# First FFN over all tile pairs, then mixer and second FFN per tile, with the instruction order fixed by a list scheduler

## The chip, the cores and the metric

The kernel runs on all eight cores of one Trainium2 chip. Each core works on one sequence of the batch, and all run the same program; they share no data. The time of a run is the device time of the slowest core, in microseconds. A profile shows the slowest core of one execution.

The program has two states. In the slow one, the cores of a die, sometimes of both, show a lower granted TensorE clock and the time is some per cent longer. A run counts as slow when one die is over 1% longer than the other at a lower clock, or when it is over 1.5% above the fastest of its kernel. The medians given are of all runs of a kernel, and where slow ones are among them, the median of the fast ones alone lies at most 1.3 us lower (for the kernel before, 15 us: 3,231.0).

## The reference

One sequence is 4,096 tokens of width 1,024. Cut to what matters:

```python
mod = silu(c) @ w_mod + b_mod               # c: one vector per sequence; 9 parts of 1,024
h = rmsnorm(x, g1) * (1 + sc1) + sh1
x = x + 0.5 * gt1 * swiglu(h, w_ffn1_in, w_ffn1_out)        # hidden width 2816
h = rmsnorm(x, g_mix) * (1 + sc2) + sh2
u_val, u_gate, u_x, u_y = split(h @ w_in)                    # 4 x 512
y_conv = silu(layernorm(causal_conv31(u_val * sigmoid(u_gate))))   # depthwise
xr = causal_conv4(u_x); r = sigmoid(xr @ w_a + b_a); i = sigmoid(xr @ w_i + b_i)
a = exp(8 * r * logsigmoid(lam)); h_t = a_t * h_{t-1} + sqrt(1 - a_t^2) * i_t * xr_t
x = x + gt2 * (concat(y_conv, gelu(u_y) * h_t) @ w_out)
x = x + 0.5 * gt3 * swiglu(rmsnorm(x, g2) * (1 + sc3) + sh3, w_ffn2_in, w_ffn2_out)
return rmsnorm(x, g_final) * (1 + f_sc) + f_sh               # silu(c) @ w_fmod
```

The convolution and the recurrence carry state along the sequence, so the mixer must go tile by tile. The first FFN depends on no other tile.

## The kernel before

A tile is 512 tokens; there are eight. Activations lie with features on the 128 partitions, so a product is a chain of 128x512 matmuls that accumulate in a PSUM bank. Weights come through four slots of 128 x 8 x 512 bf16 (1 MB). The whole layer is run tile by tile; a second tile is begun early and fills in. Tile 0 loads the fp32 weights with a cast on the POOL queue and writes the bf16 copies back to DRAM for the later tiles.

```python
def issue_slab():                       # cut
    elif tile == 0:                     # fp32 -> bf16 in flight, then written back
        emit(PL, mk(pieces), writes=[r_slot[si]], dma=sem_slot_pl[si], ...)
        emit(SP, mk(back), reads=[r_slot[si]], writes=[r_scr[pos]], dma=sem_wb[si], ...)
    else:
        emit(SP, mk(pieces), reads=[r_scr[pos]], writes=[r_slot[si]], dma=sem_slot[si], ...)

def mod_part(g0, g1):                   # modulation: one-column fp32 matmuls
    ...
    for sub in range(2):
        for kc in range(8):
            h.matmul(ps[:, bank, j:j + 1], lhsT=sf[:, kc, sub * 128:(sub + 1) * 128],
                     rhs=cact[:, kc:kc + 1], start=(kc == 0), stop=(kc == 7))

def rsqrt_chain(buf, res, bank, scale): # rstd of every norm
    E(ACT, ... func=AF.Sqrt, bias=EPS, scale=scale)
    E(DVE, ... h.reciprocal(out=buf[:], in_=buf[:]))

def conv_chunk(c):                      # conv31: 31 diagonal matmuls of 512 columns
    mm_group(b, [(dflat[:, k * 128:(k + 1) * 128], ub[:, c, k:k + T]) for k in range(NCONV)], ...)

def tile_gen(i):                        # cut: one tile, start to end
    norm(s, gs1, sh1); ffn(s, "w1i", "w1o", gth1)
    norm(s, gs2, sh2); mixer(s)
    norm(s, gs3, sh3); ffn(s, "w2i", "w2o", gth3); final norm
```

## Time and profile before

| | before |
|---|---|
| median of the three runs shown with it, two of them slow | 3,331.65 us (3,228 to 3,597) |
| median of all five | 3,246.2 us |
| span of the profiled (fast) execution | 3,239.8 us |
| PE busy | 2,835 us, 88% |

The first view is the table of windows of core 1, for four stretches. Its columns are the stretch, its length, PE's busy time with the number of matmuls in it, the granted TensorE clock, the DMA engines' mean share of busy time, and GB/s.

```profile
core 1: us, PE busy (x), PEclk, DMA share, GB/s
240.00:320.00 80.00, 75.44 (x339) 0.73 1.01 211
880.00:960.00 80.00, 72.16 (x337) 0.65 0.74 195
1040.00:1120.00 80.00, 80.00 (x372) 1.00 0.50 152
1280.00:1360.00 80.00, 80.00 (x372) 1.00 0.48 149
```

An undisturbed stretch holds 372 matmuls in 80 us, or 215.2 ns each, at clock 1.00. That is the rate that everything is measured against. Note that 240 to 320 is "94% busy" and still completes only 339, at clock 0.73: a busy share hides a clock that has dropped, so count matmuls. There the DMA share is at its limit (1.01).

The next lines are groups of instructions: line, engine and operation, output from inputs, shapes, count, then busy us and mean ns, then idle time of the engine before them and what ended most of it.

```profile
L353 PE MATMUL ps<-sb_hb,sb_slab 128*128 128x512 bf16 x7168 | 1603.8, 386 | 185.3 <-ACT sb_hb L428 77.8
...
L371 PE MATMUL ps<-sb_cact,sb_slab 128*128 128x1 f32 x1408 | 293.8, 347 | 41.4 <-DMA sb_slab<-w_mod 33.9
...
L353 PE MATMUL ps<-sb_ub,sb_slab 128*128 128x512 bf16 x992 | 217.3, 379 | 3.3 <-DMA sb_slab<-dcw 3.3
...
L394 DVE RECIPROCAL sb_rstd<-sb_rstd 128x512 f32<-128x512 f32 x32 | 107.3, 3353 | 102.5 <-ACT sb_rstd L392 102.5
```

The second line is the modulation: 1,408 matmuls that make one column each. The fourth is the reciprocal of a 128x512 tile, 3.35 us, in the chain from one norm to the next matmul. The busy time of matmuls in this view is not a cost by itself, because the mean of 386 ns overlaps with neighbours; the rate of 215.2 ns is.

The last is the chain that ended last, as shares of the span by engine.

```profile
PE 71%; DMA 12%; ACT 7%; DVE 6%; issue 3%; SPq 0%; POOL 0%; ACTq 0%; DVEq 0%; POOLq 0%
```

TensorE leads, with 12% of DMA. In the windows, the stretch from 132 to 1,008 us (tile 0 with its casts) has clock 0.81 and DMA share 0.81; the later tiles lose about 45 us each in gaps at norms.

### The profile page before, as it was taken

What the parts mean: (1) busy time and instruction counts of PE and PEld (TensorE: products, weight loads), DVE (VectorE), ACT (ScalarE), POOL (GpSimd) and SP (SyncE); (2) the same over time, 40 slices, a digit from 0 to 9 for tenths busy, and PEclk for the clock granted to TensorE, in tenths of its full rate; (3) what the DMA queues carried; (4) which work ended last, traced back from release to release, by engine and by line L of the source; (5) the groups of instructions that cost most, each with busy time, mean ns of one, the idle gap of its engine ahead of it and who ended that gap; (6) DMA issues with size and microseconds to landing.
All of it is one profiled execution on the core that took longest, in us unless ns stands there. A gap on an engine that the chain in (4) does not pass through costs nothing.

```text
span 3239.8 us, 35643 instructions; the slowest of 8 cores (3213.5 to 3239.8 us)
## 1 busy us (share of the span) xinstructions
PE 2835.0 (88%) x12768; PEld 1413.3 (44%) x12768; DVE 1005.6 (31%) x1411; ACT 937.8 (29%) x1406; POOL 101.4 (3%) x146
## 2 busy tenths in 40 slices
PE   6479998797997999969979999969979999879976
PEld 6136644653572434434434444424424444334433
DVE  0210124243004123254433223355232222554232
ACT  0310215143005132164323223246132321535121
POOL 1000000001000000000000000000000000000000
PEclk9887798689768999989989999989989999989988
DMA  7699469569964465433445555433444644424442
GB/s 179 119 201 220 144 144 227 152 135 193 213 186 143 150 179 149 153 103 116 131 139 156 156 172 149 144 94 117 150 143 150 208 137 147 132 90 136 144 130 85
DMA packets 650859, 487.04 MB, mean 150 GB/s; under 512 B 11712, under 2 KB 637888, under 8 KB 650688
## 3 DMA queue, kind: packets, MB, share of 16 engines
q1 hardware_dynamic: 574944, 405.99, 42.4%
q0 software_dynamic: 75744, 78.78, 13.7%
q8 instruction: 106, 1.74, 0.2%
q14 instruction: 65, 0.53, 0.1%
HBM read 468.21 MB, written 61.73 MB: 164 GB/s over the span
## 4 chain that ended last, share of the span: by engine, by line
PE 71%; DMA 12%; ACT 7%; DVE 6%; issue 3%; SPq 0%; POOL 0%; ACTq 0%; DVEq 0%; POOLq 0%
PE ps L353 62%; PE ps L371 9%; DMA sb_xT<-x 2%; DMA sb_slab<-w_mod 2%; DVE sb_xr L489 1%; DMA sb_slab<-win 1%; DMA sb_slab<-w1i 1%; DMA sb_slab<-w2i 1%; DMA sb_slab<-w1o 1%; ACT sb_hb L428 1%; ACT sb_xsq L410 1%; DVE sb_ntmp L425 1%; DVE sb_rstd L394 1%; DMA b2i<-sb_slab 1%; DMA b1i<-sb_slab 1%
## 5 line engine op out<-in xcount | busy, mean ns | idle before, releaser
L353 PE MATMUL ps<-sb_hb,sb_slab 128*128 128x512 bf16 x7168 | 1603.8, 386 | 185.3 <-ACT sb_hb L428 77.8
L353 PEld LDWEIGHTS ps<-sb_hb,sb_slab 128*128 128x128 bf16 x7168 | 708.8, 99 | 1064.7 <-issue 252.3
L353 PE MATMUL ps<-sb_hid,sb_slab 128*128 128x512 bf16 x2816 | 614.9, 381 | 0.4 <-DMA sb_slab<-w2o 0.4
L448 DVE TENSOR_TENSOR sb_hid<-ps,sb_sgb 128x512 bf16<-128x512 f32 x352 | 240.5, 689 | 890.2 <-PE ps L353 724.8
L446 ACT ACTIVATE sb_sgb<-ps 128x512 f32<-128x512 f32 x352 | 206.0, 595 | 979.0 <-PE ps L353 976.9
L353 PEld LDWEIGHTS ps<-sb_hid,sb_slab 128*128 128x128 bf16 x2816 | 276.5, 98 | 335.9 <-issue 7.1
L371 PE MATMUL ps<-sb_cact,sb_slab 128*128 128x1 f32 x1408 | 293.8, 347 | 41.4 <-DMA sb_slab<-w_mod 33.9
L371 PEld LDWEIGHTS ps<-sb_cact,sb_slab 128*128 128x128 f32 x1408 | 293.8, 326 | 43.5 <-issue 43.2
L410 ACT ACTIVATE sb_xsq<-sb_xT 128x512 bf16<-128x512 f32 x256 | 144.1, 621 | 472.5 <-PE ps L353 207.3
L465 DVE SCALAR_TENSOR_TENSOR sb_xT<-ps,sb_gth,sb_xT 128x512 f32<-128x512 f32 x128 | 96.1, 751 | 498.6 <-PE ps L353 498.6
L353 PE MATMUL ps<-sb_ub,sb_slab 128*128 128x512 bf16 x992 | 217.3, 379 | 3.3 <-DMA sb_slab<-dcw 3.3
L428 ACT ACTIVATE sb_hb<-sb_ntmp,sb_modv 128x512 bf16<-128x512 f32 x192 | 133.4, 721 | 200.1 <-DVE sb_ntmp L425 199.1
L353 PE MATMUL ps<-sb_xsq,sb_ones_bf 128*128 128x512 bf16 x256 | 90.6, 422 | 104.6 <-ACT sb_xsq L410 101.7
L353 PEld LDWEIGHTS ps<-sb_ub,sb_slab 128*128 128x128 bf16 x992 | 96.1, 97 | 122.0 <-issue 4.2
L425 DVE SCALAR_TENSOR_TENSOR sb_ntmp<-sb_xT,sb_gs,sb_rstd 128x512 f32<-128x512 f32 x192 | 136.9, 747 | 15.8 <-ACT sb_hb L428 11.3
L394 DVE RECIPROCAL sb_rstd<-sb_rstd 128x512 f32<-128x512 f32 x32 | 107.3, 3353 | 102.5 <-ACT sb_rstd L392 102.5
L480 ACT ACTIVATE sb_ux<-ps 128x512 f32<-128x512 f32 x32 | 19.1, 598 | 314.5 <-PE ps L353 314.5
L239 POOL DMA_DIRECT2D y<-sb_oT x64 | 34.7, 542 | 2313.5 <-ACT sb_xsq L410 1629.5
L378 DVE TENSOR_TENSOR sb_modv<-ps,sb_vecs 128x16 f32<-128x16 f32 (+1 forms) x7 | 1.2, 171 | 326.3 <-PE ps L371 326.3
L353 PEld LDWEIGHTS ps<-sb_xsq,sb_ones_bf 128*128 128x128 bf16 x256 | 25.5, 100 | 165.0 <-issue 148.7
L489 DVE SCALAR_TENSOR_TENSOR sb_xr<-sb_ux,sb_vecs,sb_xr 128x512 f32<-128x512 f32 x96 | 72.1, 751 | 10.4 <-DVE sb_xr L489 0.5
L637 DVE SCALAR_TENSOR_TENSOR sb_xT<-ps,sb_modv,sb_xT 128x512 f32<-128x512 f32 x64 | 48.1, 751 | 83.6 <-PE ps L353 83.6
(77 smaller groups left out, 925.9 us busy)
## 6 DMA issues: line engine op xcount, KB each, us to landing
sb_slab<-b1i SPq DMA_DIRECT2D x154, 512.0 KB, 5.0
sb_slab<-b2i SPq DMA_DIRECT2D x154, 512.0 KB, 4.8
sb_slab<-w_mod SPq DMA_DIRECT2D x36, 1024.0 KB, 9.5
sb_slab<-b1o SPq DMA_DIRECT2D x28, 1024.0 KB, 5.8
sb_slab<-b2o SPq DMA_DIRECT2D x28, 1024.0 KB, 5.2
sb_slab<-bdc SPq DMA_DIRECT2D x28, 992.0 KB, 4.8
sb_xT<-x POOLq DMA_DIRECT2D x8, 2048.0 KB, 13.4
y<-sb_oT POOLq DMA_DIRECT2D x64, 256.0 KB, 2.4
```

What stands on the lines that cost most here:

```text
L239: return emit(eng, lambda h: [h.dma_start(out=out_ap, in_=in_ap)], reads=reads, writes=writes, dma=sem)
L353: out.append(h.matmul(ps[:, bank, :], lhsT=l, rhs=r, start=(first and idx == 0), stop=(last and idx == n - 1)))
L371: out.append(h.matmul(ps[:, bank, j:j + 1], lhsT=sf[:, kc, sub * 128:(sub + 1) * 128], rhs=cact[:, kc:kc + 1], start=(kc == 0), stop=(kc = ...
L394: E(DVE, lambda h: [h.reciprocal(out=buf[:], in_=buf[:])], reads=[res], writes=[res])
L410: E(ACT, lambda h, q=q, fc=fc: [h.activation(out=xsq[q][:], in_=xT[:, fc, :], func=AF.Square)], reads=[r_xT[fc]], writes=[r_xsq[q]])
L425: E(DVE, lambda h, q=q, fc=fc: [h.scalar_tensor_tensor(out=ntmp[q][:], in0=xT[:, fc, :], scalar=gs[:, fc:fc + 1], in1=rstd[:], op0=ALU.mul ...
L428: E(ACT, lambda h, q=q, fc=fc: [h.activation(out=hb[:, fc, :], in_=ntmp[q][:], func=AF.Identity, bias=sh[:, fc:fc + 1], scale=1.0)], reads ...
L446: E(ACT, lambda h, q=q, bg=bg: [h.activation(out=sgb[q][:], in_=ps[:, bg, :], func=AF.Silu)], reads=[r_bank[bg]], writes=[r_sgb[q]])
L448: E(DVE, lambda h, q=q, bu=bu, cg=cg: [h.tensor_tensor(out=hid[:, cg, :], in0=ps[:, bu, :], in1=sgb[q][:], op=ALU.mult)], reads=[r_bank[bu ...
L465: E(DVE, lambda h, fc=fc, b=banks[oc]: [h.scalar_tensor_tensor(out=xT[:, fc, :], in0=ps[:, b, :], scalar=gth[:, fc:fc + 1], in1=xT[:, fc, ...
L489: E(DVE, lambda h, c=c, k=k: [h.scalar_tensor_tensor(out=xr[c][:], in0=ux[:, c, k:k + T], scalar=vecs[:, V_RCW + 4 * c + k:V_RCW + 4 * c + ...
L637: E(DVE, lambda h, fc=fc, b=b: [h.scalar_tensor_tensor(out=xT[:, fc, :], in0=ps[:, b, :], scalar=gt2[:, fc:fc + 1], in1=xT[:, fc, :], op0= ...
```

## The change

Its intent: give TensorE less to do, and never let it wait. Four things come together.

1. The modulation moves to VectorE: the kernel multiplies a 128x1024 slab of transposed weights by a broadcast row and lets the instruction sum along the row.
2. The convolution handles even and odd tokens as two phases of 64 channels each. It needs 8 x 16 matmuls of 256 columns per tile instead of 124 of 512.
3. The first FFN is done for all eight tiles first, two tiles per weight slab; its result goes to DRAM and comes back for the mixer. Slabs are now ten of 128x2048 bf16 (512 KB). The weights of mixer and second FFN are cast meanwhile, DRAM to DRAM, by 54 transfers on POOL's queue; those of the first FFN are cast during pair 0, as before.
4. All operations are recorded with a duration and a priority (a lower number is more urgent), and a list scheduler fixes the order of each engine. The semaphores are then derived from what each operation reads and writes.

Rsqrt becomes exp and ln, sigmoid becomes tanh. The core of the diff, with cuts:

```diff
-def mod_part(g0, g1): ... h.matmul(ps[:, bank, j:j + 1], lhsT=..., rhs=cact[:, kc:kc + 1], ...)
+def mods(m, afters):
+    for q in range(8):
+        dma("SP", lambda b=b: b.ap.bitcast(F32), lambda s=src: s, 1 << 19, slot_sem(b), [], [b], slab=True,
+            after=(afters[q],), prio=P.prio)
+        ... h.scalar_tensor_tensor(out=w, in0=w, scalar=1.0, in1=crow.ap, op0=ALU.mult, op1=ALU.mult, accum_out=o)
-    mm_group(b, [(dflat[:, k * 128:(k + 1) * 128], ub[:, c, k:k + T]) for k in range(NCONV)], ...)
+    mms(bank, [(... slab.ap[:, s * 128:(s + 1) * 128], ... ub_t[:, g, 15 - s:271 - s]) for s in range(16)],
+        [slab, ub[g]], cols=256, sub=slice(256 * hh, 256 * hh + 256))
 ...
+for pi, tiles in enumerate(pairs):                 # first FFN
+    P.prio = 500 + pi * 100
+    lp = -25 if pi == 0 else 400 + pi * 100
+    xss = [load_x(x_dr, t, prio=... lp, after=(prev_in,)) for t in tiles]
+    hbs = [norm(xs, M_SC1, M_SH1, after=(last_in,)) for xs in xss]
+    ...                                            # 22 w1i slabs, 12 w1o slabs, each for both tiles
+psem = [VB(ap=None) for _ in range(8)]
+for n, (nm, r) in enumerate(prep):                 # 54 casts of later weights
+    a = mid[min(len(mid) - 1, n * len(mid) * 9 // (len(prep) * 10))]   # a matmul group of pairs 1 to 3
+    dma("PL", lambda d=d: d.ap, lambda src=src: src, 3 << 19, lambda n=n: psems[n % 8], [], [d, psem[n % 8]], after=(a,),
+        prio=450 + n)
+def mix_ffn2(t):
+    P.prio = 1000 + 10 * t
+    ...                                            # mixer
+    P.prio = 1100 + 10 * t
+    hb2 = norm(xs, M_SC3, M_SH3)
+    ...                                            # second FFN, final norm
 ...
+class Program: ...
+        op.after = [a for a in after if a is not None]
+def schedule(prog, ...):
+        ds = set(op.deps) | set(op.after)          # both decide the place in the list
+            if op in q.deps:                       # but only deps delay the operation
+                q.ready = max(q.ready, op.end)
```

`after` puts an operation behind another in the list. And `psem[n % 8]` makes cast n wait for cast n - 8, so up to eight casts may be in flight.

## The prediction

> **What bounds it now.** TensorE, with holes. In the table of windows, undisturbed 80 us stretches (1040:1120, 1280:1360) hold 372 matmuls at granted clock 1.00: 215.2 ns per 128x512 matmul, on all eight cores. The Trainium skill (TensorE: Matmul & The Clock Gate, Part 1) expects 13/16 clock once three cores of a die run dense matmuls; this fast trace disagrees (1.00). Groups by line: 11,360 bf16 matmuls x 0.2152 = 2,445 us, plus 1,408 one-column fp32 modulation matmuls (54.7 us per 256 in the chain of waits) = 301 us. Span 3,240, so about 494 us are waits and cold clock. The chain gives PE 71%, DMA 12%, ACT 7%, DVE 6%.
> Where: until 1,008 us tile 0 casts weights and loads w_mod; DMA share is about 1.0 in 160:320, and the clock falls to 0.63-0.8. About 210 us are lost. Afterwards two tiles take 697 us (1,008, 1,707, 2,404, 3,096) and need 2x1,412x0.2152 = 608: 45 us lost per tile, in gaps of 15-18 us at rstd (sqrt, 3.35 us reciprocal, eight scaling steps) and at the mixer's LayerNorm (table loads of 1.28 us, 17 us idle before the output projection).
>
> **The change.**
> - Modulation off TensorE: -301 us. It becomes 88 VectorE operations on 128x1024 fp32, estimated 1.3-1.5 us each (twice the 0.69-0.75 us of 128x512 operations), about 120 us in all; only the first 16 precede a matmul, behind 8.4 MB of loads.
> - Block conv: per tile 128 matmuls of 256 columns instead of 124 of 512. If each takes half of 215 ns (weight load 98 ns, so barely), 26.7 -> 14 us: -100 us in all.
> - Remaining TensorE work: 10,880 equivalents x 0.2152 = 2,341 us.
> - Reciprocal and sqrt go to exp/ln, sigmoid to tanh: reciprocals (134 us VectorE) and most of 113 table loads disappear.
> - List order lets mixer t+1 fill around FFN2 of tile t; gaps of 45 us per tile should shrink to about 5.
> - First FFN by pairs halves its weight reloads; all weight rows become contiguous; 32 MB for storing and reloading x is added.
>
> **Sum.** Start until dense matmuls about 50 us (10.5 MB; before: 132). First pair's FFN1: 227 us of matmuls, but about 65 MB of casts, write-backs, modulation and x; the saturated stretch before moved some 255 GB/s counting cast sources, so about 265 us. Pairs 1-3: 681 us of matmuls with 165 MB beside them (245 GB/s, tight): 700. Eight mixer/FFN2 tiles at 177 = 1,419, with 1.5% stalls 1,440. Tail 22. Fast run about 2,480.
>
> The times before (3,228, 3,332, 3,597) say the slow state is common; a denser kernel feels it more. Predicted 2,530 us for the median, 80% range 2,435 to 2,740. Faster by over 2%: 0.97; within 2%: 0.02; slower: 0.01.
>
> **What would show it.** fp32 matmuls gone; PE busy 93% or more of the span; 372 matmuls per 80 us after about 320 us; clock 1.00 there; a DMA share near 1 and the only large PE holes in the first 320 us; conv matmuls spaced near 108 ns.
>
> **What would make it wrong.** Continuous dense work could draw the lower clock even in fast runs (0.81 would give 2,880 and more). The order is fixed from planned times: a late w_mod load would hold VectorE in order, fill PSUM and stop TensorE, in pairs 0-3. Casts may starve first-FFN slabs. 256-column matmuls may cost more than half.

## The result, and the profile after

| | before | after |
|---|---|---|
| median of five runs | 3,246.2 us | 2,748.81 us |
| range | 3,228.41 to 3,596.71 | 2,747.94 to 2,840.53 |
| ratio of fast runs | | 0.8489 (95%: 0.846 to 0.8517) |

A ratio compares fast runs alone, so it is not quite the ratio of the medians. The output is correct. The change is 15% faster in time, but 2,749 us lies just above the predicted range of 2,435 to 2,740, and 270 us above the sum for a fast run.

The busy times and the chain that ended last, as on the page of the kernel after:

```profile
PE 2403.1 (87%) x11179; PEld 1121.6 (41%) x11392; DVE 985.2 (36%) x1632; ACT 982.6 (36%) x1538; POOL 114.5 (4%) x221
...
PE 78%; ACT 6%; SPq 6%; DMA 4%; issue 3%; DVE 2%; POOL 0%; DVEq 0%; ACTq 0%; POOLq 0%
```

PE is busy 87%, where 93% or more was predicted. The table of windows by stage on core 2 has busy us of each engine with instruction counts, then the clock, the DMA share and GB/s:

```profile
core 2: us, PE busy (x) PEld busy (x) DVE busy (x) ACT busy (x) POOL busy (x), PEclk, DMA share, GB/s
0.00:66.00 66.00, 9.22 (x16) 1.68 (x16) 27.40 (x60) 23.13 (x35) 2.99 (x9) 1.00 0.97 267
66.00:299.00 233.00, 231.86 (x1050) 105.28 (x1072) 56.46 (x85) 40.66 (x69) 25.53 (x49) 1.00 0.88 210
299.00:1160.00 861.00, 704.03 (x3148) 316.70 (x3209) 234.37 (x368) 145.62 (x239) 51.43 (x100) 0.91 0.70 162
1160.00:2724.00 1564.00, 1456.04 (x6961) 697.40 (x7089) 660.84 (x1111) 764.61 (x1184) 30.27 (x57) 0.97 0.49 161
2724.00:2747.00 23.00, 1.94 (x9) 0.58 (x6) 6.14 (x9) 8.59 (x12) 4.28 (x8) 0.61 0.25 92
```

| stage | predicted | measured | difference |
|---|---|---|---|
| start until dense matmuls | 50 | 66 | +16 |
| first FFN, pair 0 | 265 | 233 | -32 |
| first FFN, pairs 1 to 3 | 700 | 861 | +161 |
| eight tiles of mixer and second FFN | 1,440 | 1,564 | +124 |
| tail | 22 | 23 | +1 |
| sum | 2,477 (given as about 2,480) | 2,747 | +270 |

Nearly all of the miss is in two stages. The stretch in which casts, write-backs and modulation all press at once (66 to 299) is not one of them: PE is busy there 231.86 of 233 us.

The groups that answer to those of before:

```profile
L418 PE MATMUL ps<-sb_h,sb_slab 128*128 128x512 bf16 x9783 | 2206.8, 385 | 255.5 <-DMA sb_slab<-b_w1i 124.5
...
L474 DVE SCALAR_TENSOR_TENSOR sb_slab<-sb_slab,sb_crow 128x1024 f32<-128x1024 f32 x88 | 107.1, 1217 | 83.0 <-DMA sb_slab<-wmod 81.8
...
L418 PE MATMUL ps<-sb_ub,sb_slab 128*128 128x256 bf16 x1024 | 116.1, 273 | 9.5 <-ACT sb_c L390 9.4
```

The one-column matmuls are gone. The modulation costs VectorE 107 us at 1,217 ns each, where 1.3 to 1.5 us had been estimated; in the chain that ended last, the loads of its weights have only 0.9%. The 256-column matmuls again have a mean that overlaps; in the timeline, the stretch of one tile's convolution shows their real spacing (start, length, engine, instructions):

```profile
1651.14 7.17 PE L418 MATMUL ps<-sb_ub,sb_slab 128*128 128x256 bf16 x64
```

7.17 us over 64 is 112 ns, about half of 215. So these parts came out as predicted. The waits of PE show what did not (what it waited for: us in all, times, longest us):

```profile
PE ps L418 <- DMA sb_slab<-b_w1i: 124.5, 3, 54.4
PE ps L418 <- ACT sb_h L390: 124.1, 31, 16.2
PE ps L418 <- DVE sb_c L394: 35.4, 7, 10.1
PE ps L418 <- ACT sb_c L390: 23.5, 15, 2.0
```

### Pairs 1 to 3: late slabs

Pieces of the chain that ended last, in order of time (start us, length us, what):

```profile
332.94 48.54 SPq L425
387.90 11.60 DMA sb_slab<-b_w1i
...
919.64 48.81 DMA sb_slab<-b_w1i
...
1693.91 11.99 PE ps L418 x47
...
1884.81 11.99 PE ps L418 x47
```

Around 330 to 400 us the chain is the sequencer of the SP queue, then one DMA of a `b_w1i` slab; the hole near 920 is a slab DMA of 48.8 us alone. (The other two pieces, 190.9 us apart, are the same place in two successive tiles, so a tile's period is 191 us where its matmuls need 177.) The timeline of POOL for the same time:

```profile
297.95 3.91 POOL L425 DMA_DIRECT2D b_win<-win  x8
308.72 0.49 POOL L425 DMA_DIRECT2D b_dcw<-dcw  x1 [6.86 <-DMA b_win<-win]
```

Eight casts leave in 3.9 us, the moment that POOL is free of pair 0's stores; each next leaves as soon as the cast eight before it lands. They were meant to be spread over three pairs. Nothing holds them, because `after` is no wait. The timeline of the SP queue:

```profile
306.34 81.47 SPq L425 DMA_DIRECT2D sb_c<-x  x16
387.90 1.19 SPq L425 DMA_DIRECT2D sb_slab<-b_w1i  x2
```

The sixteen loads of x for the next pair (256 KB each) take 81 us to issue, and the slabs that TensorE needs now stand behind them in order. The view of the DMA queues between 310 and 380 us (packets, MB, share of the 16 engines' time):

```profile
q0 software_dynamic: 458, 7.50, 95.1%
q1 hardware_dynamic: 426, 0.80, 4.8%
```

POOL's software queue has 95.1% of the engines' time. The hardware queue, with x, the slabs and the modulation weights, gets 4.8%. Dividing MB by packets, a cast's packet has 16 KB and the other queue's 2 KB. The Trainium skill (Trainium Kernel Development and Optimization, Key Constraints) says that DMAs issued from the SP, ACT and POOL queues share the same 16 engines and interleave; this trace agrees that they share, and shows how unevenly. The packets of the two queues, on the other hand, are nearly one for one: 458 to 426. Three such holes, around 305 to 400, 610 to 702 and 905 to 968 us, hold 532 matmuls in 250 us, where 250 / 0.2152 = 1,162 would fit (some 2% of this core's matmul records are missing; the holes are as deep on other cores). The granted clock in them is lower too (0.70, 0.74 and 0.85).

### Mixer tiles: a norm that comes too late

The timeline of VectorE between the mixer of one tile and its second FFN:

```profile
1518.57 0.75 DVE L394 SCALAR_TENSOR_TENSOR sb_c<-ps,sb_modv,sb_c 128x512 f32<-128x512 f32 x1 [0.98 <-PE ps L418]
...
1526.00 5.39 DVE L394 SCALAR_TENSOR_TENSOR sb_c<-sb_c,sb_gs 128x512 f32<-128x512 f32 x8 [1.25 <-ACT sb_c L390]
...
1620.17 5.39 DVE L394 SCALAR_TENSOR_TENSOR sb_c<-sb_c,sb_gs 128x512 f32<-128x512 f32 x8 [3.62 <-ACT sb_c L390]
...
1681.21 1.41 DVE L394 SCALAR_TENSOR_TENSOR sb_c<-sb_c,sb_gs 128x512 f32<-128x512 f32 x2 [0.24 <-ACT sb_c L390]
...
1691.62 3.39 DVE L394 SCALAR_TENSOR_TENSOR sb_c<-sb_c,sb_gs 128x512 f32<-128x512 f32 x5
```

The last residual of the mixer of this tile, t, is written at 1,518.57. The scaling for the norm before its second FFN begins at 1,681, 163 us later. In between stand the final norm of tile t-2 (1,526; the first stores of y follow it), the second FFN of tile t-1, whose matmuls begin at 1,518, and the norm of the next mixer (1,620). All have more urgent priorities: 1100 + 10(t-2), 1100 + 10(t-1) and 1000 + 10(t+1) against 1100 + 10t. So when the serial steps of the next mixer come, no second FFN is ready to fill in, and TensorE waits for them, for instance 4.22 us before the output projection at 1,693.91. In the view of PE's waits above, these are the lines on `sb_c`: from 1,300 to 2,600 us, PE waits 55.4 us on `sb_c` and only 2.2 us on `sb_h`. The 124.1 us on `sb_h` belong to the start and the first FFN (85.4 us before 1,160) and to the first tiles after it.

### The profile page after: what moved, and what is told of

Same layout as the page of the kernel before. It is cut to its first block, busy times and chain, and to the rows that moved or that the text cites. A ratio compares the mean times of both kernels' runs of the same rounds, so it can differ in the third digit from the quotient of the medians.

```text
span 2746.4 us, 34315 instructions; the slowest of 8 cores (2738.7 to 2746.4 us)
## 1 busy us (share of the span) xinstructions
PE 2403.1 (87%) x11179; PEld 1121.6 (41%) x11392; DVE 985.2 (36%) x1632; ACT 982.6 (36%) x1538; POOL 114.5 (4%) x221
## 4 chain that ended last, share of the span: by engine, by line
PE 78%; ACT 6%; SPq 6%; DMA 4%; issue 3%; DVE 2%; POOL 0%; DVEq 0%; ACTq 0%; POOLq 0%
PE ps L418 78%; SPq L425 6%; ACT sb_c L390 4%; DMA sb_slab<-b_w1i 3%; ACT sb_h L390 1%; DVE sb_c L394 1%; DMA sb_slab<-wmod 1%; ACT L390 1%; DVE sb_c L398 0%; DMA sb_c<-xmid 0%; DVE sb_slab L474 0%; DVE sb_h L408 0%; POOL y L425 0%; DVEq L111 0%; ACTq L111 0%
## 5 line engine op out<-in xcount | busy, mean ns | idle before, releaser
L418 PE MATMUL ps<-sb_h,sb_slab 128*128 128x512 bf16 x9783 | 2206.8, 385 | 255.5 <-DMA sb_slab<-b_w1i 124.5
L418 PEld LDWEIGHTS ps<-sb_h,sb_slab 128*128 128x128 bf16 x9984 | 985.9, 99 | 1457.8 <-issue 317.3
L390 ACT ACTIVATE sb_c<-ps 128x512 f32<-128x512 f32 x400 | 237.0, 596 | 1076.1 <-PE ps L418 1053.6
L398 DVE TENSOR_TENSOR sb_h<-ps,sb_c 128x512 bf16<-128x512 f32 x352 | 242.8, 691 | 942.5 <-PE ps L418 863.3
L390 ACT ACTIVATE sb_h<-sb_c 128x512 bf16<-128x512 f32 x288 | 172.7, 624 | 337.6 <-DVE sb_c L394 198.8
L394 DVE SCALAR_TENSOR_TENSOR sb_c<-sb_c,sb_gs 128x512 f32<-128x512 f32 x256 | 173.2, 745 | 62.7 <-ACT sb_c L390 62.7
L418 PE MATMUL ps<-sb_h,sb_ones 128*128 128x512 bf16 x309 | 98.0, 393 | 57.4 <-ACT sb_h L390 53.5
L474 DVE SCALAR_TENSOR_TENSOR sb_slab<-sb_slab,sb_crow 128x1024 f32<-128x1024 f32 x88 | 107.1, 1217 | 83.0 <-DMA sb_slab<-wmod 81.8
L390 ACT ACTIVATE sb_h<-sb_c,sb_modv 128x512 bf16<-128x512 f32 x192 | 126.4, 716 | 20.9 <-DVE sb_c L394 11.4
L418 PE MATMUL ps<-sb_ub,sb_slab 128*128 128x256 bf16 x1024 | 116.1, 273 | 9.5 <-ACT sb_c L390 9.4
```

The source lines that it names most:

```text
L390: return A("ACT", dur, lambda: (lambda o, i: (lambda h: [h.activation(out=o, in_=i, func=func, bias=bias, scale=scale)]))(out(), in_()), r ...
L394: return A("DVE", dur, lambda: (lambda o, a, b: (lambda h: [h.scalar_tensor_tensor(out=o, in0=a, scalar=scalar, in1=b, op0=op0, op1=op1)]) ...
L398: return A("DVE", dur, lambda: (lambda o, a, b: (lambda h: [h.tensor_tensor(out=o, in0=a, in1=b, op=op)]))(out(), in0(), in1()), reads, wr ...
L418: return [h.matmul(o, lhsT=l, rhs=r, start=(first and i == 0), stop=(last and i == n - 1)) for i, (l, r) in enumerate(pr)]
L474: return lambda h: [h.scalar_tensor_tensor(out=w, in0=w, scalar=1.0, in1=crow.ap, op0=ALU.mult, op1=ALU.mult, accum_out=o)]
```

## The experiments

The theories and rivals have letters in the expectations.

- A: the bursts of casts crowd the slabs out in pairs 1 to 3. B, its rival: the bytes are simply too many there.
- Within A, how: A1 says that the engines take turns by packet, so the queue with small packets loses. A2, its rival, says that it is the burst, whatever its packets. A3 says that the number of casts in flight decides, and A4, its rival, that any burst hurts, because one running cast alone fills the engines. The expectations of e10 and e11 add a rival to A3, a threshold: any second cast in flight brings back the loss.
- C: the late second norm makes the gaps in the tiles. D, its rival: ScalarE is the limit there (it is busy 765 of 1,564 us). E is the rival to C where C is extended to the boundaries of the pairs: the buffers of the next pair's tiles are not free.

Medians are in us; compare with 2,748.8 and ratio 0.8489. The runs of the kernel before were shared by the kernels that ran together: e1 to e4, then e5, e6 and e9, then e10 to e12.

### e1: each cast really waits for its matmul group

The same bytes, the same list; the anchor becomes a semaphore wait.

```diff
+ def emit(eng, fn, reads=(), writes=(), dma=None, extra=()):
+     for tk in extra: need(tk)
      ...
      dma("PL", ..., [], [d, psem[n % 8]], after=(a,), prio=450 + n)
+     P.ops[-1].gate = a
      ...
-     emit(e, fn, rs, ws, dma=sm)
+     op.tok = emit(e, fn, rs, ws, dma=sm, extra=[op.gate.tok] if op.gate is not None else ())
```

> The same order on every engine as the changed kernel; only each of the 54 DRAM-to-DRAM weight casts now really waits, by a semaphore, for the first-FFN matmul group that it was anchored to. Bytes are the same. Theory A (bursts of casts, which no semaphore held back, starve the loads on the SP queue): the three holes of TensorE at the pair boundaries (about 95, 90 and 60 us near 305-400, 610-702 and 905-968) shrink to at most 25 us each, pairs 1 to 3 take about 700-740 us instead of about 860, and the kernel takes 2,600-2,650 us. Rival B (the 165 MB beside pairs 1 to 3 are simply too much for the DMA engines): the holes are spread over the pairs but their sum stays within 40 us of before, and the kernel takes 2,710-2,760 us.

Measured: 2,618.0, ratio 0.8024, so 131 us less. The stage of pairs 1 to 3 falls from 861 to 728 us. PE no longer waits for `b_w1i` at all; casts now leave one at a time, released by PE. The mixer stage stays at 1,567. The row of pairs 1 to 3 (PE only), to be read against that of the kernel after:

```profile
299.00:1027.00 728.00, 699.06 (x3213) 0.98 0.82 191
```

A holds and B falls: all the bytes still move in the shorter time, at 191 GB/s instead of 162, and the engines' share of busy time is 0.82.

### e2: small packets for the casts

The scratch rows get a pitch of 2,112 elements, so that a cast's output is no longer one contiguous piece and its packets shrink.

```diff
-    w_scr = {k: nc.dram_tensor("b_" + k, [v.shape[0], 2048], BF16, ...)
+    w_scr = {k: nc.dram_tensor("b_" + k, [v.shape[0], 2048 if k in ("w1i", "w1o") else 2112], BF16, ...)
-    scr = {k: [VB(ap=dr(w_scr[k], r)) ...
+    scr = {k: [VB(ap=dr(w_scr[k], r)[:, 0:2048]) ...
```

> The bursts of casts stay as they are, but the scratch rows get a pitch of 2,112 elements, so a cast can write at most 4 KB in one piece (its packets were 15 KB on average, those of the x loads 2 KB). Theory A1 (the engines alternate between queues by packet, so large cast packets crowd out the small loads): the 16 x loads of the second boundary take under 45 us to issue instead of 82, the holes shrink by half or more, kernel 2,620-2,690 us. Theory A2 (it is the burst, whatever its packets): issue still takes 65 us or more, kernel within 1% of 2,748 us.

Measured: 2,739.0, ratio 0.8397, 10 us less. The queues between 310 and 380 us, to be read against the same view of the kernel after:

```profile
q0 software_dynamic: 1813, 6.61, 78.7%
q1 hardware_dynamic: 1639, 3.00, 19.5%
```

Cast packets are now 3.6 KB, the other queue's share rises from 4.8% to 19.5%, and the loads of x issue in 43.9 instead of 81.5 us, as A1 expected. PE still waits 112 us for `b_w1i`, and the time is within 1% of the kernel after, as A2 had it. The Trainium skill (DMA: Bandwidth & Descriptors, Queues, rings and completion order) says each engine round-robins between the queue rows "at *packet* granularity"; the counts agree here, if the profile's packets are the page's: 458 to 426 before and 1,813 to 1,639 now. So A1 has the turns right and its time (2,620 to 2,690) wrong: with packets nearly one for one, 3.00 MB reach the other queue in these 70 us, where e5 below moves 12.43 MB. The holes stay, and smaller packets alone are not a sufficient remedy.

### e5, e10, e11: one, two or four casts in flight

No wait for TensorE; only the rotation of eight is cut. This also enters the planned list. Rebuilding the kernels gives e11 the list of the kernel after on every engine but VectorE; e5 and e10 have 105 of PE's 1,600 entries and six of SP's 786 in other places, but the same places in both (between these two, only six of VectorE's 1,544 differ). So e5 against e10 shows the number of casts alone.

```diff
-    dma("PL", ..., [], [d, psem[n % 8]], after=(a,), prio=450 + n)
+    dma("PL", ..., [], [d, psem[n % 1]], after=(a,), prio=450 + n)      # e5; n % 2 in e10, n % 4 in e11
```

> The changed kernel with one edit: the casts share one ordering buffer instead of rotating over eight, so only one cast is in flight at a time, but nothing ties them to TensorE's progress: they still run in bursts. Theory A3 (what hurts is the queue of eight casts waiting at the engines): with one in flight the loads get the engines between two casts, the holes shrink by half or more, kernel 2,640-2,690 us. Theory A4 (any burst hurts, because a running cast alone fills the engines): holes within 25% of before, kernel 2,720-2,760 us. In both cases the casts themselves take longer, about 7 us each instead of about 5.

> The changed kernel with two casts in flight in place of eight (one in flight gave 2,615 us, eight 2,748 us). Theory A3 (the number of casts that wait at the engines sets what is left for the loads): between the two and nearer to one, 2,615-2,660 us, waits of TensorE on first-FFN slabs under 40 us in total. If instead any second cast closes the gap between two casts (a threshold, not a depth): 2,700 us or more.

> The same with four in flight. Theory A3: between two and eight, 2,650-2,720 us, waits on first-FFN slabs 40 to 100 us. Threshold: the same as eight within 1%.

The queues of e5 in the same window:

```profile
q1 hardware_dynamic: 4410, 12.43, 63.9%
q0 software_dynamic: 211, 3.24, 31.2%
```

| casts in flight | time | ratio | share of the slabs' queue | PE's wait for `b_w1i` |
|---|---|---|---|---|
| 8 (after) | 2,748.8 | 0.8489 | 4.8% | 124.5 us |
| 4 (e11) | 2,754.8 | 0.8466 | 5.0% | 130.1 us |
| 2 (e10) | 2,718.8 | 0.8353 | 26.2% | 89.8 us |
| 1 (e5) | 2,615.4 | 0.8077 | 63.9% | none |

One of e10's three runs was slow (2,766). One in flight gains 133 us, better than the 2,640 to 2,690 that A3 had expected, and as much as e1's pacing; A4 falls. But a smooth dependence on depth, as A3 had it, falls too: four is no better than eight, two gives back a quarter, one gives all. The threshold came out: over 2,700 with two, within 1% of eight with four.

What e5 has and the others lack is a pause: between the end of one cast and the start of the next (one every 10 us, where casts of about 7 us had been expected), the software queue is empty. The packet counts from 310 to 380 us fit this. With eight and four in flight they are nearly one for one (458 to 426 and 448 to 418, casts first), as turns by packet give when both queues always have work. With two they are 356 to 2,453 and with one 211 to 4,410, so the slabs' queue often found no cast in its way. (In the third hole of the kernel after, without loads of x in the queue, the counts are 320 to 224 from 910 to 960 us.) That the pause is the cause remains an inference from these four points, since no view shows the queue of a single DMA engine; nor is it isolated why two in flight leave the slabs' queue only 26%.

### e3: the second norm gets the mixer's priority

```diff
-            P.prio = 1100 + 10 * t
             hb2 = norm(xs, M_SC3, M_SH3)
+            P.prio = 1100 + 10 * t
```

> One line moved: the norm before the second FFN gets the priority of the mixer instead of that of the second FFN, which runs to a higher number. Theory C (in the planned order the statistics of the next tile's norm starve behind the second FFN, so that FFN cannot fill the holes of the mixer): the period of a mixer/FFN2 tile falls from 191 us to 178-182, kernel 2,650-2,690 us. Rival D (ScalarE is the limit in the mixer stretch, 80% busy there, whatever the order): period stays 188 us or more, kernel 2,725 us or more. The holes at the pair boundaries must stay in both cases.

Measured: 2,656.0 (three fast runs; one slow at 2,971), ratio 0.8141, 93 us less. In the chain that ended last, the tiles' marks stand at 1,487.69, 1,667.79, 1,848.31, 2,028.21, 2,208.70 and 2,388.60, a period of 180.2 us instead of 191. `b_w1i` still costs 128.6 us. PE's next waits, to be read against those of the kernel after, have no line on `sb_c` from VectorE any more:

```profile
PE ps L418 <- ACT sb_h L390: 110.4, 34, 16.6
PE ps L418 <- ACT sb_c L390: 6.2, 10, 2.0
```

From 1,300 to 2,600 us all of PE's waits fall from 59.7 to 7.4 us, and the granted clock rises from 0.97 to 1.00. C holds. D falls: ScalarE does the same work in less time.

### e4: both

The edits of e1 and e3 together.

> The paced casts and the earlier norm together. If theories A and C both hold and act in different stages, the gains add: 2,748 less the gains of the two single runs, to within 15 us; about 2,520-2,580 us by the numbers above. If B and D hold: 2,690 us or more.

Measured: 2,519.3 (one slow run, 2,829), ratio 0.7721, 229.5 us less; e1 and e3 alone give 131 + 93 = 224. The two causes add up, so they are separate. The stages are 66, 233, 728, 1,468 and 23 us. What is left of pairs 1 to 3 can be seen in windows around the boundaries of the pairs (columns as before, PE only):

```profile
core 4: us, PE busy (x), PEclk, DMA share, GB/s
290.00:340.00 50.00, 40.32 (x182) 0.90 0.84 188
...
780.00:840.00 60.00, 50.39 (x221) 0.91 0.60 124
```

About 10 us of PE idle at each of the boundaries, although the casts no longer come in bursts.

### e6: the next pair's norm becomes urgent

```diff
     # on top of e4
+            P.prio = 350 + pi * 100 if pi else 500
             hbs = [norm(xs, M_SC1, M_SH1, after=(last_in,)) for xs in xss]
+            P.prio = 500 + pi * 100
```

> On top of paced casts and the earlier second norm: the norm of the next pair in the first-FFN stage also gets a number below that of the pair before, so that its statistics no longer wait until that pair's matmuls are used up. Theory C, generalised: the 12 us holes that are left at each of the three pair boundaries (period 242.5 us for 230 us of matmuls) go, three times 10-12 us, kernel 2,480-2,495 us against 2,519. Rival E (the holes are there because the buffers for the next pair's normalised tiles are not free): kernel 2,510-2,525 us.

Measured: median 2,525.2, ratio 0.7798; fast runs 2,498 to 2,525, slow ones 2,759 and 2,900. By the time alone this missed the 2,480 to 2,495 of the theory and looks no better than e4. But the cores of one run differ. In four of the five fast runs the slowest cores (2,515 to 2,524 us) have a mean clock of 0.968 to 0.979, while the other cores of the same run have 0.98 to 0.99 and take 2,478 to 2,499 us; in e4's fast runs every core took 2,511 to 2,518. In the profiled run, of 2,498 us, the slowest core is held up otherwise, by two waits for `b_w1i` of 7.2 us together and the clock after them. On its core 1, the fastest (2,477.2 us), the same windows read:

```profile
core 1: us, PE busy (x), PEclk, DMA share, GB/s
290.00:340.00 50.00, 50.00 (x233) 1.00 0.94 227
...
780.00:840.00 60.00, 60.00 (x280) 1.00 0.82 198
```

The holes are gone, and pairs 1 to 3 take 691 us instead of 728. C extended to the boundaries holds, and E falls, on the undisturbed cores; the time of the chip does not show it here.

### e9: the first mixer begins before the first FFN ends

```diff
     # on top of e6
-            P.prio = 1000 + 10 * t
+            P.prio = 1000 + 10 * t if t else 790
```

> As the run before, and the first tile's mixer gets a priority number below that of the last pair's first FFN, so that it runs among that pair's matmuls. The stretch between the last first-FFN matmul and the steady state (about 1,027 to 1,150 us in the paced run with early norm) loses some 25-35 us of holes: kernel 2,450-2,475 us. If the mixer's matmuls then delay the first FFN by as much as they fill, within 10 us of the run before.

Measured: fast runs 2,467 to 2,498, median 2,494.9 with a slow one of 2,559; ratio 0.7685. Again three of the four fast runs lie above the 2,450 to 2,475 expected. In the profiled run, cores 6 and 7 took 2,493 and 2,492 us; the others 2,453 to 2,464. Cores 6 and 1 in one window:

```profile
core 6: us, PE busy (x), PEclk, DMA share, GB/s
350.00:400.00 50.00, 49.65 (x188) 0.81 0.83 194
```

```profile
350.00:400.00 50.00, 50.00 (x233) 1.00 1.00 227
```

Core 6 is as busy as core 1 but completes 188 matmuls where core 1 completes 233, at clock 0.81 (some 2% of core 6's records are missing). So the kernel's own time is that of the undisturbed cores, within the expectation. Most of the rest is clock: from 340 to 515 us core 7 completes 671 matmuls and core 1 812, a loss of 141 x 0.2152 = 30 us of the 38 between them. But five cores, 0, 2, 4, 6 and 7, also wait 5.5 to 8.0 us for `b_w1i` before it. Cores 1, 3 and 5, without that wait, took 2,453 to 2,454 us, and cores 0, 2 and 4, with it but at clock 1.00 afterwards, 2,461 to 2,464.

### e12: all that helped, with one cast in flight instead of pacing

The edits of e5, e3, e6's norm priority and e9's mixer priority; no wait of POOL for PE.

> The simplest version with all that the runs pointed to: one cast in flight and no semaphore to TensorE, and the three priority edits. 2,455-2,475 us on undisturbed cores; if the pacing to TensorE was needed as well, 2,490 us or more.

Measured: 2,458.6 (four fast runs, 2,456.6 to 2,459.6), ratio 0.7556. That is 0.89 of the time of the kernel after, and the shortest of all. The other expectation, 2,490 us or more if the pacing by TensorE was needed as well, did not come. The page's line of busy time:

```profile
PE 2357.0 (96%) x11178; PEld 1112.6 (45%) x11392; DVE 981.5 (40%) x1632; ACT 997.9 (41%) x1553; POOL 114.6 (5%) x221
```

PE is busy 96%, its clock is 0.98 to 1.00 in the dense stages, and its remaining waits for `sb_h` are 68.7 us, from 124.1, with 58.8 of them before 300 us. The stages, cut at the same places as in e6, are 66, 233, 691, 1,440 and 29 us. The cut at 990 us no longer divides the work: the first mixer runs among pair 3, whose last `b_w1o` slabs are issued at 1,008 us. Only the sum of the two, 2,131 us, can be compared. In all four runs, every core took 2,451 to 2,458 us at a mean clock of 0.986 to 0.997. In the profiled run none of the cores waits for `b_w1i`, where five cores of e6's profile and five of e9's do. The runs don't show whether e12 was spared the lower clocks of e6 and e9 because of that or by chance.

## Why the prediction was right or wrong

The verdict (faster by over 2%, 0.97) was right. The time was 219 us above the point and 9 us above the range.

- **Right: the arithmetic.** The one-column matmuls are gone, and 112 ns for a 256-column matmul and 215 ns for the rest held. In e12, pairs 1 to 3 and the mixer tiles take 2,131 us together against 2,140 predicted, and the total is 2,458.6 against about 2,480. The sum was a good sum for a kernel whose order worked, and it took the edits of e12, one of which (the first mixer begun early) was no part of it, to get one. There is some luck in it: the start is 16 us too short in the sum and pair 0 is 32 us too long.
- **Right, with a reserve: the clock.** In the profile of the kernel after, pair 0 ran at 0.99 or 1.00 on all eight cores. The Trainium skill (TensorE: Matmul & The Clock Gate, Part 1) would have given 13/16; the prediction went with the trace of before and was right for this kernel. The lower clock in a fast run, named as a risk, did appear in e9, with 0.81 from about 340 to 510 us on two cores; that denser work draws it is not shown.
- **Wrong: "Pairs 1-3: 681 us of matmuls with 165 MB beside them (245 GB/s, tight): 700."** This term measured 861. It counted the bytes of the whole stage over its time, as if the casts were spread over it and the slabs got their share. The bytes were counted rightly: 162 GB/s x 861 us is 139 MB, and 54 casts whose sources are 0.5 MB larger than their outputs bring it to 166. But the casts came in three bursts that left the slabs' queue 4.8% of the engines in the first hole. e1 moved the same bytes through this stage in 133 us less, so the bytes were not the limit; the queue was. The text does not say whether it took `after` for a wait. It named "Casts may starve first-FFN slabs" as a risk but gave it no cost, although the missing wait could have been read in the code.
- **Wrong: "gaps of 45 us per tile should shrink to about 5", hence "1.5% stalls".** They shrank to about 14 (191 less 177). The step took for granted that the list order would have work for every gap. Here it did so only while work was left, and a priority that puts the norm of a tile behind the second FFN of the tile before and the next mixer used it up too early. e3 gets the gap to 3.2 (180.2 less 177) with one moved line.
- **Wrong: "the only large PE holes in the first 320 us" and "PE busy 93% or more".** Both follow from the two above. The first 320 us, feared as the worst, were nearly free of holes from 66 to 299: pair 0 took 233 us, 32 less than the term.
- **A smaller miss: the start.** 66 us instead of 50. At 267 GB/s for 66 us some 17.6 MB were moved before dense work, not 10.5: the second tile's x, more of the modulation weights and the first cast slabs with their write-backs are among them.

What stays open: the cause of the steep step between one and two casts in flight, and what triggers the stretches at clock 0.81. Untested is also a remedy on the other side: the sixteen loads of x stand before the slabs in SP's list by their priority, and no run moved them behind.

## What to carry to other kernels

An order in a list is not a wait: if background transfers must not run ahead, let a semaphore hold them, or allow one in flight so that the urgent queue finds the engines free; cost a stage's DMA by who stands in which queue, not by bytes alone. A scheduler's priorities should make the short serial preparation of the next dense stage (a norm) more urgent than any bulk work, since its value is not its own time but the matmuls it releases. When a predicted sum is missed, take the profile by stage and undo one cause at a time; here the two main causes gave 131 and 93 us alone and 229.5 together.

## What the Trainium skill lacked or had wrong

- TensorE: Matmul & The Clock Gate, Part 1: it says the whole die goes to 13/16 clock soon after a third core runs dense matmuls, and stays there while the load lasts. Here all eight cores ran dense at 1.00 for whole executions (e12, from 299 to 2,430 us: 1.00 on every core). In e9, cores 6 and 7 ran at 0.81 from about 340 to 510 us and then at 1.00 again with the load unchanged, while cores 4 and 5 of the same die were at 1.00 from 350 us on. In seven fast runs of e6 and e9 some cores have a longer span at a lower mean clock, each time in neighbouring pairs. The page speaks of the default power profile; the runs don't show which was set.
- DMA: Bandwidth & Descriptors, Queues, rings and completion order: turns by packet fit the packet counts of the saturated windows (458 to 426, of 16 and 2 KB). The page does not say how the shares depend on how much one queue has in flight: a queue of DRAM-to-DRAM casts took about 95% of the engines' time with four or eight in flight, 69% with two and 31% with one (the other queue: 5%, 26%, 64%). It gives no advice to cap background transfers at one.
- No page read says that the cost of a blocked hardware queue shows as the issue time of the SP sequencer: sixteen loads of 256 KB took 81.5 us to issue, 43.9 us with smaller cast packets, and 28.7 us with two casts in flight.
